# A hybrid decoder layer on one core: first weights loaded in quarters, the output gate's weights prepared in twos, convolutions one column later, half of the down projection's sums later

## The chip, the core and the metric

The kernel runs on one core of a Trainium2 chip. Five engines work beside each other and meet only through semaphores: TensorE (PE: matmuls, with its weight loads as PEld), VectorE (DVE), ScalarE (ACT), GpSimd (POOL) and SyncE (SP), which here issues nearly all transfers. Each engine takes its instructions strictly in the order in which the built program has them, so one that has to wait holds up all behind it. The metric is the time of one execution in microseconds on the device (us). Less is better.

## The reference, cut to what matters

```python
hn   = rmsnorm(x, attn_norm_w)                     # x: 1024 tokens x 1024
proj = hn @ w_in                                   # 3592 columns
da_q, da_k, da_v, ml_qk, ml_v, ml_o, ml_i, ml_f = split_projection(proj)
da   = rmsnorm(diff_attention(da_q, da_k, da_v, lam, slopes), diff_norm_w) * (1 - lam_init)
qk   = silu(causal_dwconv(ml_qk, mlstm_conv_w, mlstm_conv_b))     # width 4, 1024 channels
mq, mk = split(qk)
h    = mlstm_chunkwise(mq, mk * 128**-0.5, ml_v, ml_i + b_i, log_sigmoid(ml_f + b_f))
mix  = concat(da, sigmoid(ml_o) * rmsnorm(h, mlstm_norm_w))
x    = x + mix @ w_out
u    = causal_dwconv(rmsnorm(x, ffn_norm_w) @ w_up, ffn_conv_w, ffn_conv_b)
gate, up = split(u)
x    = x + (silu(gate) * up) @ w_down              # 2816 hidden channels
return rmsnorm(x, final_norm_w)
```

All of it is in float32. The change touches only the first fifth of the program, from the first load to the value projections. What it computes stays the same.

## The kernel before

A float32 factor is split into a high part (rounded to the matmul's type, `fp32r`, on ACT) and a low part (the rest, by a subtraction on DVE or POOL), and each product is three matmuls of 128x128 by 128x512: high x high, high x low, low x high. L158 to L160 (`mm3`) and L163 to L165 (`mm3b`) are these three. `split` (L115 and L116) makes the two parts of half a piece of weights, `split_x` (L212, L213) those of x.

The first fifth of the program runs in this order on PE:

1. eleven idle matmuls (L233) that keep PE at work until data arrives;
2. columns ct = 0 to 3 of `ml_qk` (queries of the mLSTM) for the first half of the tokens (`banks(0)`: the four accumulators in the two `big` tiles of PSUM), then for the second half (`banks(1)`: `mm`, `mm`, `sa`, `sb`). Each half is 4 columns x 8 slices kc of the model dimension x 3 matmuls. Before the change the order is: slices 0 to 3 of columns 0 and 1, slices 0 to 3 of columns 2 and 3, then slices 4 to 7 of all four. So the first load brings the first half (512 wide, 256 KB) of the weights of columns 0 and 1 (`col_halves`);
3. columns ct = 4 to 7 (keys), two halves each, in PSUM tiles that rotate (`rotate`);
4. the gate's pre-activations: 16 matmuls into a small PSUM tile `sb` and 16 into `sa` (L411), each copied to `gs` by L412;
5. the units of the output gate, `o_unit(0)` to `o_unit(7)`, then those of the attention's values, `v_unit(0)` to `v_unit(7)`, each 24 matmuls; `filler` puts small steps of the mLSTM's gates between them (eight transposes of `gs`, L477, after the second unit);
6. the projection of the mLSTM's values (first two tiles into `sa` and `sb`), and the chunks.

PSUM tiles `sa` and `sb` are taken in turn by `small`. A taker waits until the last holder was copied out: the copies of the keys are L393 on ACT, those of the queries L374 and L379.

Behind the matmuls run the convolutions of the 8 columns. M[ct] is first multiplied by the tokens' scale RB on DVE (L387, L394). `conv_qk(ct)` is one ACT instruction (L361) and three taps on DVE (L363, 128x1021 to 1023 elements) into an accumulator of the tag `ta` (4 buffers), and `silu_qk(ct)` one on ACT (L366).

POOL meanwhile makes sums of blocks of `w_down` for a later Strassen product. `down_sums` loads a pair (2 x 512 KB), makes 4 subtractions of 128x512 on POOL (L327), and `store_sums` writes the pair to memory (L333). There are 11 pairs. Their buffers are `vda` in the columns' loop, and `ta` in `late_sums`; `first_up_sums` does the same for two pairs of `w_up` (L341 to L344). Before the change a pair stands at ct = 1, 3, 4, 5, 6 and 7, at o_unit 1, 3, 5 and 7, and at v_unit 0.

Weights of 1024 columns go through one of two buffers `wf` and are split into two of eight tiles `w` (`wpiece`; `getw` takes the next of a list). `wo` are the four pieces of the output gate, `wv` those of the attention's values, and four more (`w_mv` too) are those of the mLSTM's values. A load into `wf` waits until its last content was split. A split waits until PE has used the `w` tile's last content.

A scheduler orders the instructions of every engine by dependencies and priorities, so an engine's order is not just that of the code. SP carries all loads and stores in one order: a store that waits for POOL holds up each load behind it.

Of the kernel before, what the change touches and what calls it, by code (L numbers as in the profile page):

```python
# [10 lines left out]
F32 = mybir.dt.float32  # L11
F32R = mybir.dt.float32r
I32 = mybir.dt.int32
AF = mybir.ActivationFunctionType
ALU = mybir.AluOpType
PSUM = bass.MemoryType.PSUM

P = 128
S = 1024
D = 1024  # L20
NT = S // P
KC = D // P
# [17 lines left out]
def tile_hybrid(ctx: ExitStack, tc: tile.TileContext, I: dict, out: bass.AP):  # L40
    nc = tc.nc
    V = nc.vector
    A = nc.scalar
# [23 lines left out]
    wp = Scope("wp")  # L67
# [34 lines left out]
    first = cp.tile([P, 1], F32, name="first")  # L102
# [9 lines left out]
    def split(dst, src, loeng, scale=None):  # L112

        if scale is None:
            A.activation(dst[:, 0, :], src, AF.Copy)  # L115
            loeng.tensor_tensor(dst[:, 1, :], src, dst[:, 0, :].bitcast(F32), op=ALU.subtract)  # L116
        else:
            A.activation(dst[:, 0, :], src, AF.Copy, scale=scale)
            V.scalar_tensor_tensor(dst[:, 1, :], src, scale, dst[:, 0, :].bitcast(F32), op0=ALU.mult, op1=ALU.subtract)

    def wtile():
        return wp.t([P, 2, 512], F32R, "w", 8)

    HV = (slice(0, 512), slice(512, 1024))
# [21 lines left out]
    def getw(ahead):  # L146
        n = used[0]
        used[0] += 1
        while len(made) < min(n + 1 + ahead, len(specs)):
            made.append(wpiece(*specs[len(made)]))  # L150
        return made[n]
# [48 lines left out]
    def load_x(i, hf, between=None):  # L200
        f = pa.t(XS, tag="ta", bufs=4)
        for c in ([slice(0, 1), slice(1, 2)] if between else [slice(0, 2)]):
            nc.sync.dma_start(f[:, c, :], I["xT"][:, 2 * i + c.start:2 * i + c.stop, HV[hf]])
            if between and c.start == 0:
                between()
        return f

    def split_x(i, hf, f):
        hi, lo = (px.t(XS, F32R, "xb", 16) for _ in range(2))
        for c in range(2):  # L210
            k = 2 * i + c
            A.activation(hi[:, c, :], f[:, c, :], AF.Copy, scale=anw[:, k:k + 1])  # L212
            V.scalar_tensor_tensor(lo[:, c, :], f[:, c, :], anw[:, k:k + 1], hi[:, c, :].bitcast(F32), op0=ALU.mult, op1=ALU.subtract)  # L213
        xb[i, hf] = hi, lo
# [15 lines left out]
    cw = {}  # L230
# [1 line left out]
    for _ in range(11):  # L232
        PE.matmul(idle, ones, ones, start=True, stop=True)  # L233

    def col_halves(half, *cts, first=False):

        f = wp.t([P, 1024], F32, "wf", 2)
        for ct, t in zip(cts, HV):
            nc.sync.dma_start(f[:, t], I["w_st"][ct][:, HV[half]])
            yield  # L240
            w = cw[ct, half] = wtile()
            if first:
                V.tensor_copy(w[:, 0, :], f[:, t])
                V.tensor_tensor(w[:, 1, :], f[:, t], w[:, 0, :].bitcast(F32), op=ALU.subtract)
            else:
                split(w, f[:, t], V)

    def col_piece(ct):
        cw[ct, 0], cw[ct, 1] = wpiece(I["w_st"][ct], None, V)

    g0 = col_halves(0, 0, 1, first=True)
    f = load_x(0, 0, lambda: next(g0))
    next(g0)
    split_x(0, 0, f)
    f = load_x(1, 0)
    split_x(1, 0, f)
    for _ in g0:
        pass
    for _ in col_halves(0, 2, 3):
        pass  # L260
    f = load_x(2, 0)
    split_x(2, 0, f)
    for _ in col_halves(1, 0, 1):
        pass
    f = load_x(3, 0)
    split_x(3, 0, f)
    for _ in col_halves(1, 2, 3):
        pass
    nc.sync.dma_start(cst, I["cst"])
    nc.sync.dma_start(wg, I["wg"])  # L270
    for i in range(4):
        f = load_x(i, 1)
# [39 lines left out]
    gs = pa.t([16, S], tag="gs")  # L312
# [6 lines left out]
    def down_sums(alloc=lambda: pr0.t([P, S], tag="vda", bufs=4), n=1):  # L319
        h0, h1 = HV  # L320
        for i in (pairs.pop(0) for _ in range(min(n, len(pairs)))):
            g, u = (alloc() for _ in range(2))
            for k, f in enumerate((g, u)):
                nc.sync.dma_start(f, I["w_down"][2 * i + k])
            for dst, x_, y in ((g[:, h1], g[:, h1], g[:, h0]), (u[:, h1], u[:, h1], g[:, h1]),
                               (u[:, h0], u[:, h0], u[:, h1]), (g[:, h0], u[:, h1], g[:, h0])):
                GP.tensor_tensor(dst, x_, y, op=ALU.subtract)  # L327
            dsum.append((i, g, u))

    def store_sums(n=1):  # L330
        for i, g, u in (dsum.pop(0) for _ in range(min(n, len(dsum)))):
            for k, f in enumerate((g, u)):
                nc.sync.dma_start(usum[i - NJ, k] if i >= NJ else wsum[i, k], f)  # L333

    def first_up_sums(j):

        h0, h1 = HV
        g, u = (pa.t([P, S], tag="ta", bufs=4) for _ in range(2))
        for k, f in enumerate((g, u)):
            nc.sync.dma_start(f, I["w_up"][j, k])  # L340
        GP.tensor_tensor(u[:, h0], g[:, h0], u[:, h0], op=ALU.subtract)  # L341
        GP.tensor_tensor(u[:, h1], u[:, h1], u[:, h0], op=ALU.subtract)
        GP.tensor_tensor(g[:, h0], u[:, h1], g[:, h0], op=ALU.add)
        GP.tensor_tensor(g[:, h1], g[:, h1], u[:, h1], op=ALU.subtract)  # L344
        dsum.append((NJ + j, g, u))

    def tok(tiles, tt):
        return tiles[tt // 2][:, tt % 2, :]

    def col_mm(ps, ct, kc, hf):  # L350
        k = slice(kc % 4 * P, (kc % 4 + 1) * P)
        w = cw[ct, kc // 4]
        mm3(ps, w[:, 0, k], w[:, 1, k], *xpart(kc, hf), kc == 0, kc == KC - 1)
# [3 lines left out]
    def conv_qk(ct):  # L357

        u = M[ct]
        acc = cacc[ct] = pa.t([P, S], tag="ta", bufs=4)  # L360
        A.activation(acc, u, AF.Identity, bias=mcb[:, ct:ct + 1], scale=mcw[:, ct, 3:4])  # L361
        for d in (1, 2, 3):
            V.scalar_tensor_tensor(acc[:, d:], u[:, :S - d], mcw[:, ct, 3 - d:4 - d], acc[:, d:], op0=ALU.mult, op1=ALU.add)  # L363

    def silu_qk(ct):
        A.activation(M[ct], cacc.pop(ct), AF.Silu)  # L366

    pss = banks(0)
    for cts, kcs in (((0, 1), range(4)), ((2, 3), range(4)), (range(4), range(4, 8))):
        for kc in kcs:  # L370
            for ct in cts:
                col_mm(pss[ct], ct, kc, 0)
    for ct in range(4):
        A.activation(M[ct][:, HV[0]], pss[ct], AF.Copy)  # L374
    pss = banks(1)
# [9 lines left out]
    stats()  # L385
    for ct in range(4):
        V.tensor_tensor(M[ct], M[ct], RB, op=ALU.mult)  # L387
    for ct in range(4, 8):
        for hf in range(2):
            ps = rotate(2 * ct + hf)  # L390
            for kc in range(KC):
                col_mm(ps, ct, kc, hf)
            A.activation(M[ct][:, HV[hf]], ps, AF.Copy)  # L393
        V.tensor_tensor(M[ct], M[ct], RB, op=ALU.mult)  # L394
        store_sums()
        down_sums()
        if ct == 4:
            col_piece(7)
        elif ct == 6:
            wo = [getw(0) for _ in range(4)]  # L400
        conv_qk(ct - 4)
        if ct > 4:
            silu_qk(ct - 5)
    mq, mk = M[0:4], M[4:8]


    for hf in range(2):
        gp = small([16, 512])
        for kc in range(KC):
            for m, x_ in enumerate(xpart(kc, hf)):  # L410
                PE.matmul(gp, wg16[:, kc, :], x_, start=(kc, m) == (0, 0), stop=(kc, m) == (KC - 1, 1))  # L411
        V.tensor_copy(gs[:, HV[hf]], gp)  # L412
    conv_qk(4)
    silu_qk(3)

    def mv_mm(ps, w, tt):
        for kc in range(KC):
# [6 lines left out]
    def late_sums():  # L424
        store_sums()
        down_sums(lambda: pa.t([P, S], tag="ta", bufs=4))
# [7 lines left out]

    def o_unit(tt):
        store_sums()
        if tt < 4:
            if tt < 3:
                conv_qk(5 + tt)
            silu_qk(4 + tt)  # L440
        if tt % 2:
            late_sums()
        if tt == 5:
            wv.extend(getw(0) for _ in range(4))
        if tt == NT - 1:
            return
        tts = (tt,) if tt < NT - 2 else (tt, tt + 1)
        pss = [rotate(k) for k in tts]
        mv_pair(pss, wo, tts)
        for ps, k in zip(pss, tts):  # L450
            A.activation(tok(Tt, k), ps, AF.Tanh, scale=rstdh[:, k:k + 1])

    def v_unit(tt):
        store_sums()
        if tt in (2, 4):
            first_up_sums(tt // 2 - 1)
        if tt == 0:
            late_sums()
            vda.extend(pr0.t([P, 2, 512], tag="vda", bufs=4) for _ in range(4))
        if tt == NT - 1:  # L460
            return
        tts = (tt,) if tt < NT - 2 else (tt, tt + 1)
        pss = [rotate(k + 2) for k in tts]
        mv_pair(pss, wv, tts)
        for ps, k in zip(pss, tts):
            A.activation(tok(vda, k), ps, AF.Copy, scale=rstd[:, k:k + 1])
# [184 lines left out]
    w = [getw(1) for _ in range(4)]  # L651
# [706 lines left out]
```

## Time and profile before

| | |
|---|---|
| median of 3 runs | 1214.32 us (1213.82 to 1214.63) |
| profiled execution, its own time | 1213.26 us |
| its span in the trace | 1211.5 us |
| PE busy / PEld busy | 1183.0 us (98%) / 973.3 us (80%) |
| DVE / ACT / POOL busy | 899.2 us (74%) / 571.0 us (47%) / 480.1 us (40%) |
| mean granted clock of TensorE | 0.995 of full speed |

The profiled execution took 1213.26 us by the clock that timed the runs; its trace spans 1211.5 us, and what is between them is start and end. It is one of the faster executions. Times in the text are microseconds from the start of the span. PE is busy nearly always, so the kernel can become faster only where PE waits or runs at a lower clock.

### The profile page before, as it was taken

The page shows a single profiled execution, that of the slowest core. Times are in us where ns is not written, and L with a number is a line of the kernel's source. Part 1 is how long each engine was busy: PE and PEld are TensorE (multiplying, and loading weights), DVE is VectorE, ACT ScalarE, POOL GpSimd, SP SyncE. Part 2 cuts the span into 40 slices and gives each one's busy share as a digit, 9 for nine tenths or more (in the row PEclk, how much of TensorE's full clock was granted, in tenths as well). Part 3 has the DMA queues.
Part 4 walks back from the last instruction along what each step waited for, and adds up shares of the span by engine and source line. Part 5 has one row for each costly group of instructions (what it writes and reads, how often), then busy time and mean ns, then how long its engine had stood idle before and what let it go on. Part 6 is the DMA issues. An engine that isn't in the chain of part 4 may idle for free.

```text
span 1211.5 us, 15939 instructions
## 1 busy us (share of the span) xinstructions
PE 1183.0 (98%) x5622; PEld 973.3 (80%) x5622; DVE 899.2 (74%) x1564; ACT 571.0 (47%) x1114; POOL 480.1 (40%) x364
## 2 busy tenths in 40 slices
PE   9998999999999999999999999999999999999996
PEld 7885788888778878888888888888888888888885
DVE  5598232566767777669998998788887878886694
ACT  6534323334666666344644444434344345544462
POOL 0475451003543431001198887888887600000000
PEclk9998999999999999999999999999999999999999
DMA  8755664124212243332322312222222169823223
GB/s 307 252 206 205 226 243 166 62 71 157 79 52 54 70 157 114 121 127 99 124 70 87 103 72 100 91 70 87 77 80 104 54 217 346 296 96 96 96 79 139
DMA packets 61743, 159.03 MB, mean 131 GB/s; under 512 B 6176, under 2 KB 10464, under 8 KB 61664
## 3 DMA queue, kind: packets, MB, share of 16 engines
q1 hardware_dynamic: 61232, 157.21, 38.0%
q8 instruction: 44, 0.72, 0.3%
q10 hardware_dynamic: 432, 0.82, 0.2%
q14 instruction: 35, 0.29, 0.1%
HBM read 116.02 MB, written 37.78 MB: 127 GB/s over the span
## 4 chain that ended last, share of the span: by engine, by line
PE 84%; DVE 5%; DMA 3%; ACT 3%; POOL 3%; issue 1%; SPq 1%; POOLq 0%; ACTq 0%; DVEq 0%
PE mm L160 6%; PE mm L158 6%; PE mm L159 6%; PE mm L163 5%; PE mm L164 5%; PE mm L165 5%; PE big L158 4%; PE big L160 4%; PE big L159 4%; PE big L164 4%; PE big L165 4%; PE big L163 4%; PE sb L777 3%; POOL vda L327 3%; PE sb L158 2%; PE sb L160 2%
## 5 line engine op out<-in xcount | busy, mean ns | idle before, releaser
L115 ACT ACTIVATE w<-wf 128x512 fp32r<-128x512 f32 x160 | 97.7, 624 | 142.3 <-POOL wf L999 33.6
L116 DVE TENSOR_TENSOR w<-wf,w 128x512 fp32r<-128x512 f32 x128 | 108.4, 858 | 27.9 <-ACT w L115 21.7
L1041 DVE SCALAR_TENSOR_TENSOR y<-x2b,fcw,y 128x1022 f32<-128x1022 f32 x44 | 91.8, 2125 | 0.0
L1040 DVE SCALAR_TENSOR_TENSOR y<-x2b,fcw,y 128x1023 f32<-128x1023 f32 x44 | 75.7, 1762 | 9.4 <-ACT y L1039 9.4
L116 POOL TENSOR_TENSOR w<-s,w 128x512 fp32r<-128x512 f32 x40 | 69.8, 1746 | 6.2 <-ACT w L115 6.2
L327 POOL TENSOR_TENSOR vda<-vda 128x512 f32<-128x512 f32 x24 | 46.6, 1958 | 63.7 <-DMA vda<-in_w_down_dram 62.9
L116 POOL TENSOR_TENSOR w<-wf,w 128x512 fp32r<-128x512 f32 x32 | 46.9, 1469 | 57.0 <-ACT w L115 47.2
L116 POOL TENSOR_TENSOR w<-wu,w 128x512 fp32r<-128x512 f32 x40 | 66.5, 1662 | 1.8 <-ACT w L115 1.8
L158 PE MATMUL mm<-xb,w 128*128 128x512 f32 x168 | 66.1, 394 | 0.0
L160 PE MATMUL mm<-xb,w 128*128 128x512 f32 x168 | 65.9, 392 | 0.0
L159 PE MATMUL mm<-xb,w 128*128 128x512 f32 x168 | 65.9, 392 | 0.0
L968 POOL TENSOR_TENSOR s<-wu 128x512 f32<-128x512 f32 x20 | 36.5, 1825 | 58.0 <-DMA wu<-in_w_up_dram 58.0
L752 DVE CUSTOM_DVE_ANT_0 s<-big,B 128x128 f32<-128x128 f32 (+7 forms) x64 | 47.6, 755 | 13.7 <-PE big L750 12.3
L1039 ACT ACTIVATE y<-x2b,fcw 128x1024 f32<-128x1024 f32 x44 | 52.3, 1237 | 9.6 <-DVE x2b L1030 8.4
L754 ACT ACTIVATE s<-s,mb 128x128 f32<-128x128 f32 (+7 forms) x64 | 49.3, 772 | 11.2 <-DVE mb L753 10.0
L163 PE MATMUL big<-w 128*128 128x512 f32 x132 | 51.5, 390 | 0.8 <-DVE x L1202 0.8
L164 PE MATMUL big<-w 128*128 128x512 f32 x132 | 51.4, 389 | 0.0
L165 PE MATMUL big<-w 128*128 128x512 f32 x132 | 51.3, 389 | 0.0
L115 ACT ACTIVATE w<-wu 128x512 fp32r<-128x512 f32 x48 | 29.7, 625 | 40.1 <-PE mm L160 10.7
L777 PEld LDWEIGHTS sb<-vda,aT 128*128 128x128 f32 x288 | 36.2, 190 | 15.4 <-ACT aT L774 14.6
L777 PE MATMUL sb<-vda,aT 128*128 128x128 f32 x288 | 44.2, 289 | 3.7 <-ACT aT L774 3.1
L115 ACT ACTIVATE w<-hb 128x512 fp32r<-128x512 f32 x41 | 25.8, 630 | 44.9 <-PE big L165 19.8
(514 smaller groups left out, 3769.8 us busy)
## 6 DMA issues: line engine op xcount, KB each, us to landing
wf<-in_w_up_dram SPq DMA_DIRECT2D x22, 512.0 KB, 4.5
actd<-y SPq DMA_DIRECT2D x21, 512.0 KB, 2.6
wu<-in_w_up_dram SPq DMA_DIRECT2D x20, 512.0 KB, 3.4
wf<-in_w_st_dram SPq DMA_DIRECT2D x12, 512.0 KB, 4.2
vda<-in_w_down_dram SPq DMA_DIRECT2D x12, 512.0 KB, 6.6
wsum<-vda SPq DMA_DIRECT2D x12, 512.0 KB, 3.0
wf<-in_w_mv_dram SPq DMA_DIRECT2D x12, 512.0 KB, 5.3
wf<-wsum SPq DMA_DIRECT2D x12, 512.0 KB, 3.4
```

Of the source, the lines that this page charges most:

```text
L115: A.activation(dst[:, 0, :], src, AF.Copy)
L116: loeng.tensor_tensor(dst[:, 1, :], src, dst[:, 0, :].bitcast(F32), op=ALU.subtract)
L158: PE.matmul(ps, sh, mh, start=first, stop=False)
L159: PE.matmul(ps, sh, ml, start=False, stop=False)
L160: PE.matmul(ps, sl, mh, start=False, stop=last)
L163: PE.matmul(ps, sh, w[:, 0, :], start=first, stop=False)
L164: PE.matmul(ps, sl, w[:, 0, :], start=False, stop=False)
L165: PE.matmul(ps, sh, w[:, 1, :], start=False, stop=last)
L327: GP.tensor_tensor(dst, x_, y, op=ALU.subtract)
L777: PE.matmul(ops, aT[:, b * P:(b + 1) * P], vda[k // 2][:, k % 2, h * P:(h + 1) * P], start=k == 0, stop=k == qt)
L1040: V.scalar_tensor_tensor(y[:, 1:], u[:, :S - 1], cw[:, 1:2], y[:, 1:], op0=ALU.mult, op1=ALU.add)
L1041: V.scalar_tensor_tensor(y[:, 2:], u[:, :S - 2], cw[:, 0:1], y[:, 2:], op0=ALU.mult, op1=ALU.add)
```

## The change

- **First weights in quarters.** Two steps of `first_quarter` load 256 columns (128 KB) of the weights of all four columns, instead of two steps of `col_halves` that load 512 columns of two of them. Every part is now split on ACT and DVE by `split`; the first two were made on DVE alone (L243, L244). PE takes the first half of the tokens slice by slice over all four columns.
- **Output gate's weights in twos.** Two pieces are prepared in the step ct = 6 and two in ct = 7, ahead of that step's sums and convolution, instead of four in ct = 6.
- **Convolutions a column later.** `conv_qk(0)` stands in the step ct = 5, not 4, and so on. All silus stand in the units of the output gate.
- **The copies of the gate's pre-activations** move from DVE (L412) to ACT.
- **Down sums.** Pairs now stand at ct = 1, 3, 5 and 7 and at o_unit 1, 3 and 5 (buffers `vda`), at o_unit 7 and at v_unit 0, 3 and 6 (`ta`).

```diff
-    g0 = col_halves(0, 0, 1, first=True)
+    def first_quarter(q):
+
+        f = wp.t([P, 1024], F32, "wf", 2)
+        for ct in range(4):
+            c, r = slice(256 * ct, 256 * (ct + 1)), slice(256 * q, 256 * (q + 1))
+            nc.sync.dma_start(f[:, c], I["w_st"][ct][:, r])
+            yield
+            if q == 0:
+                cw[ct, 0] = wtile()
+            split(cw[ct, 0][:, :, r], f[:, c], V)
+
+    g0 = first_quarter(0)
+    next(g0)
     f = load_x(0, 0, lambda: next(g0))
-    next(g0)
     split_x(0, 0, f)
+    for _ in g0:
+        pass
     f = load_x(1, 0)
     split_x(1, 0, f)
-    for _ in g0:
-        pass
-    for _ in col_halves(0, 2, 3):
+    for _ in first_quarter(1):
         pass
...
     pss = banks(0)
-    for cts, kcs in (((0, 1), range(4)), ((2, 3), range(4)), (range(4), range(4, 8))):
-        for kc in kcs:
-            for ct in cts:
-                col_mm(pss[ct], ct, kc, 0)
+    for kc in range(KC):
+        for ct in range(4):
+            col_mm(pss[ct], ct, kc, 0)
...
+    wo = []
     for ct in range(4, 8):
...
         V.tensor_tensor(M[ct], M[ct], RB, op=ALU.mult)
-        store_sums()
-        down_sums()
         if ct == 4:
             col_piece(7)
-        elif ct == 6:
-            wo = [getw(0) for _ in range(4)]
-        conv_qk(ct - 4)
+        elif ct > 5:
+            wo += [getw(0) for _ in range(2)]
+        if ct % 2:
+            store_sums()
+            down_sums()
         if ct > 4:
-            silu_qk(ct - 5)
+            conv_qk(ct - 5)
...
-        V.tensor_copy(gs[:, HV[hf]], gp)
-    conv_qk(4)
-    silu_qk(3)
+        A.activation(gs[:, HV[hf]], gp, AF.Copy)
...
     def o_unit(tt):
         store_sums()
-        if tt < 4:
-            if tt < 3:
-                conv_qk(5 + tt)
-            silu_qk(4 + tt)
-        if tt % 2:
+        if tt < 5:
+            conv_qk(3 + tt)
+        silu_qk(tt)
+        if tt in (1, 3, 5):
+            store_sums()
+            down_sums()
+        elif tt == NT - 1:
             late_sums()
...
     def v_unit(tt):
         store_sums()
         if tt in (2, 4):
             first_up_sums(tt // 2 - 1)
+        elif tt in (0, 3, 6):
+            late_sums()
         if tt == 0:
-            late_sums()
             vda.extend(pr0.t([P, 2, 512], tag="vda", bufs=4) for _ in range(4))
```

How the built program's order changes at three places:

SP, while PE works on columns 4 to 7. `wf<-in_w_st` is the piece of column 7, `wf<-in_w_mv` are the output gate's pieces, `vda<-in_w_down` and `wsum<-vda` the loads and stores of the sums. Before:

```order
L324 DMA vda<-in_w_down_dram 128x1024 x3
L333 DMA wsum<-vda 128x1024 x2
L129 DMA wf<-in_w_st_dram 128x1024
L333 DMA wsum<-vda 128x1024 x2
L324 DMA vda<-in_w_down_dram 128x1024 x4
L333 DMA wsum<-vda 128x1024 x2
L129 DMA wf<-in_w_mv_dram 128x1024 x2
```

After:

```order
L129 DMA wf<-in_w_st_dram 128x1024
L328 DMA vda<-in_w_down_dram 128x1024
L337 DMA wsum<-vda 128x1024 x2
L328 DMA vda<-in_w_down_dram 128x1024
L129 DMA wf<-in_w_mv_dram 128x1024 x2
L337 DMA wsum<-vda 128x1024 x2
L129 DMA wf<-in_w_mv_dram 128x1024
L328 DMA vda<-in_w_down_dram 128x1024 x4
L337 DMA wsum<-vda 128x1024
L129 DMA wf<-in_w_mv_dram 128x1024
```

The first two pieces of the output gate stood behind the loads of the fourth and fifth pair and the stores of the third and fourth; now they stand behind the stores of the second.

ACT, at the end of the columns, from the copy of `sa` (the first half of column 7) to the first units of the output gate (L451 before, L455 after). Before:

```order
L393 ACTIVATE mqk<-sa 128x512
L366 ACTIVATE mqk<-ta 128x1024
L115 ACTIVATE w<-wf 128x512 x2
L393 ACTIVATE mqk<-mm 128x512
L361 ACTIVATE ta<-mqk,par 128x1024
L366 ACTIVATE mqk<-ta 128x1024
L451 ACTIVATE Tt<-mm,rstdh 128x512
```

After:

```order
L397 ACTIVATE mqk<-sa 128x512
L370 ACTIVATE mqk<-ta 128x1024
L115 ACTIVATE w<-wf 128x512
L397 ACTIVATE mqk<-mm 128x512
L115 ACTIVATE w<-wf 128x512
L365 ACTIVATE ta<-mqk,par 128x1024
L416 ACTIVATE gs<-sb 16x512
L370 ACTIVATE mqk<-ta 128x1024
L416 ACTIVATE gs<-sa 16x512
L455 ACTIVATE Tt<-mm,rstdh 128x512
```

The scheduler has left the silus among the columns, and the second copy to `gs` now stands behind the last silu.

SP, while PE works on the attention's values. `mwd` and `DT` are small exchanges of the mLSTM's gates, the last `wf<-in_w_mv` rows the pieces of its values. Before:

```order
L340 DMA ta<-in_w_up_dram 128x1024 x3
L333 DMA usum<-ta 128x1024 x3
L522 DMA mwd<-s 32x128
L333 DMA usum<-ta 128x1024
L129 DMA wf<-in_w_mv_dram 128x1024
L522 DMA mwd<-s 32x128
L586 DMA DT<-mwd 128x512 x2
```

After:

```order
L328 DMA ta<-in_w_down_dram 128x1024 x2
L337 DMA usum<-ta 128x1024 x2
L337 DMA wsum<-ta 128x1024
L527 DMA mwd<-s 32x128
L337 DMA wsum<-ta 128x1024
L344 DMA ta<-in_w_up_dram 128x1024 x2
L527 DMA mwd<-s 32x128
L328 DMA ta<-in_w_down_dram 128x1024 x2
L337 DMA usum<-ta 128x1024 x2
L337 DMA wsum<-ta 128x1024 x2
L129 DMA wf<-in_w_mv_dram 128x1024
L591 DMA DT<-mwd 128x512 x2
```

Two pairs of down sums now stand here with their loads and stores, ahead of the second piece of the mLSTM's values. From there on the program's order is as before.

## Rows read from the trace of the kernel before

**Rows 1.** The page's first part: busy time, share and instructions of each engine.
```profile
PE 1183.0 (98%) x5622; PEld 973.3 (80%) x5622; DVE 899.2 (74%) x1564; ACT 571.0 (47%) x1114; POOL 480.1 (40%) x364
```

**Rows 2.** The waits of PE: total us, times, longest us.
```profile
PE sa L411 <- ACT mqk L393: 5.9, 1, 5.9
...
PE big L158 <- DVE w L243: 1.7, 2, 0.9
```

**Rows 3.** Timeline of the first 10 us, PE and DVE: start, us, instruction, idle time before it.
```profile
0.99 4.21 PE L233 MATMUL sa<-ones 128*128 128x128 f32 x22 [0.99 <-POOL wprev L544]
...
7.51 0.43 DVE L243 CAST w<-wf 128x512 fp32r<-128x512 f32 x1 [0.24 <-DMA wf<-in_w_st_dram]
...
9.06 0.39 PE L158 MATMUL big<-xb,w 128*128 128x512 f32 x1
9.29 0.39 PE L159 MATMUL big<-xb,w 128*128 128x512 f32 x1
```

**Rows 4.** Timeline of PE, 95 to 217 us.
```profile
96.09 3.88 PE L411 MATMUL sb<-xb,wg 128*16 128x512 f32 x16
105.90 5.71 PE L411 MATMUL sa<-xb,wg 128*16 128x512 f32 x16 [5.92 <-ACT mqk L393]
...
124.86 0.42 PE L477 MATMUL sb<-cst,gs 16*128 16x16 f32 x4 [2.02 <-DVE gs L412]
...
210.97 0.39 PE L165 MATMUL sa<-w,xb 128*128 128x512 f32 x1
```

**Rows 5.** Windows of 10 us: busy us of PE, PEld, DVE, ACT, POOL; PEclk.
```profile
100.00:110.00 10.00, 4.10 (x10) 1.42 (x11) 9.49 (x7) 5.36 (x7) 6.49 (x4) 0.66 0.47 191
```

**Rows 6.** Timeline of ACT, 60 to 110 us.
```profile
91.53 2.43 ACT L115 ACTIVATE w<-wf 128x512 fp32r<-128x512 f32 x4 [5.07 <-DMA wf<-in_w_mv_dram]
...
105.27 0.57 ACT L393 ACTIVATE mqk<-sa 128x512 f32<-128x512 f32 x1
```

**Rows 7.** Timeline of DVE, 50 to 210 us.
```profile
53.51 6.83 DVE L387 TENSOR_TENSOR mqk<-mqk,RB 128x1024 f32<-128x1024 f32 x4 [3.73 <-ACT RB L302]
60.27 9.00 DVE L363 SCALAR_TENSOR_TENSOR ta<-mqk,par,ta 128x1023 f32<-128x1023 f32 x4
...
92.19 3.62 DVE L116 TENSOR_TENSOR w<-wf,w 128x512 fp32r<-128x512 f32 x4 [2.35 <-ACT w L115]
95.74 4.85 DVE L363 SCALAR_TENSOR_TENSOR ta<-mqk,par,ta 128x1022 f32<-128x1022 f32 x4
...
102.87 1.22 DVE L394 TENSOR_TENSOR mqk<-mqk,RB 128x1024 f32<-128x1024 f32 x1
...
207.88 0.69 DVE L116 TENSOR_TENSOR w<-wf,w 128x512 fp32r<-128x512 f32 x1 [0.98 <-ACT w L115]
```

**Rows 8.** Timeline of POOL, 50 to 190 us.
```profile
55.05 15.36 POOL L327 TENSOR_TENSOR vda<-vda 128x512 f32<-128x512 f32 x7 [4.13 <-DMA vda<-in_w_down_dram]
77.83 16.23 POOL L327 TENSOR_TENSOR vda<-vda 128x512 f32<-128x512 f32 x8 [7.42 <-DMA vda<-in_w_down_dram]
...
166.26 3.90 POOL L327 TENSOR_TENSOR ta<-ta 128x512 f32<-128x512 f32 x3 [6.85 <-DMA ta<-in_w_down_dram]
...
185.72 1.29 POOL L344 TENSOR_TENSOR ta<-ta 128x512 f32<-128x512 f32 x1
```

**Rows 9.** Timeline of SP's queue of transfers, 60 to 215 us.
```profile
86.94 1.24 SPq L129 DMA_DIRECT2D wf<-in_w_mv_dram  x2
...
170.56 4.96 SPq L340 DMA_DIRECT2D ta<-in_w_up_dram  x3
...
187.42 0.42 SPq L129 DMA_DIRECT2D wf<-in_w_mv_dram  x1
```

**Rows 10.** Transfers issued from 145 to 190 us: count, KB each, median us to landing.
```profile
wsum<-ta SPq DMA_DIRECT2D x4, 512.0 KB, 5.0
ta<-in_w_up_dram SPq DMA_DIRECT2D x4, 512.0 KB, 4.5
usum<-ta SPq DMA_DIRECT2D x4, 512.0 KB, 2.6
```

**Rows 11.** The same view, transfers issued from 186 to 215 us.
```profile
wf<-in_w_mv_dram SPq DMA_DIRECT2D x3, 512.0 KB, 3.5
```

More of the change, by code (lines that the diff above doesn't have):

```diff
@@ L233, in tile_hybrid, with col_halves @@
         PE.matmul(idle, ones, ones, start=True, stop=True)
-    def col_halves(half, *cts, first=False):
+    def col_halves(half, *cts):
         f = wp.t([P, 1024], F32, "wf", 2)
@@ L239, in col_halves @@
             nc.sync.dma_start(f[:, t], I["w_st"][ct][:, HV[half]])
-            yield
             w = cw[ct, half] = wtile()
[L242 to L246, printed above, removed]
+            split(w, f[:, t], V)
     def col_piece(ct):
         cw[ct, 0], cw[ct, 1] = wpiece(I["w_st"][ct], None, V)
-    g0 = col_halves(0, 0, 1, first=True)
+    def first_quarter(q):
[9 more added lines that the diff above has]
+    next(g0)
     f = load_x(0, 0, lambda: next(g0))
-    next(g0)
     split_x(0, 0, f)
+    for _ in g0:
+        pass
     f = load_x(1, 0)
     split_x(1, 0, f)
-    for _ in g0:
-        pass
-    for _ in col_halves(0, 2, 3):
+    for _ in first_quarter(1):
         pass
@@ L262, in tile_hybrid @@
     split_x(2, 0, f)
-    for _ in col_halves(1, 0, 1):
-        pass
+    col_halves(1, 0, 1)
     f = load_x(3, 0)
     split_x(3, 0, f)
-    for _ in col_halves(1, 2, 3):
-        pass
+    col_halves(1, 2, 3)
     nc.sync.dma_start(cst, I["cst"])
```

## The prediction

> **What bounds the kernel.** I read the page first, then the waits of PE, then the timelines around each wait. PE is busy for 98% of the span [rows 1], and two of its waits lie where the change works: 5.9 us before the second half of the gate's matmuls, which wait for ACT's copy out of `sa`, and 1.7 us at the start [rows 2]. The reader should see three more things. After the 5.92 us wait the 16 matmuls take 5.71 us, where the 16 before it took 3.88; the granted clock is 0.66 on average from 100 to 110 us, that is, TensorE was put from its level of 2.4 GHz to 1.2 for a part of it [rows 4, 5]. That costs another 1.83 us. And the transposes of `gs` wait 2.02 us at 124.86. From there to the first bank of the mLSTM's values I found no wait of PE in the trace. So 5.92 + 1.83 + 2.02 + 1.7 = 11.5 us is all that the change can win here.
>
> Why was the copy late? SP issued the output gate's first two pieces only at 86.94, since stores of sums that waited for POOL stood ahead of them [rows 9]. ACT, which takes its work in order, waited 5.07 us for their landing until 91.53, with finished columns uncopied behind it [rows 6]. DVE in turn waited 2.35 us for ACT [rows 7]. But DVE is the longer queue: from 53.51 it works until its multiplication ends at 102.87 + 1.22 = 104.09; then ACT makes a convolution step and the copy at 105.27, done at 105.84. 50.6 us on DVE with 2.35 idle leave 48.2 us of work. It is the true bound of this wait.
>
> **First weights in quarters.** Matmuls that follow each other start 0.23 us apart, as at 9.06 and 9.29 [rows 3]. By 9.06 PE had done six, so it runs as if it had started at 9.06 - 6 x 0.227 = 7.70. The idle matmuls end at 0.99 + 4.21 = 5.20. In the new order the four quarters of slice 0 and the two slices of x are the same 1,024 KB that lay ahead of 7.51, when the second half-piece landed [rows 3]; so the last quarter is there at about 7.5. Its halves cost half of 2.43/4 on ACT [rows 6] and half of 0.69 on DVE [rows 7]: 0.3 and 0.35 us. PE then has work for 24 matmuls, of which nine need only the first three quarters, and has done 13 by about 8.7: as if from 5.75. That is a gain of 1.95 at most; 0 if the quarters land no earlier than halves did. I take 1.7. The eight more splits and four more issues lie in the gaps before x's next slices; without that cover they would cost some 2.6 us on ACT.
>
> The Trainium skill ("DMA: Bandwidth & Descriptors", Rules for kernel authors) speaks against it: it wants transfers large, 1 MiB and more, and says small ones should be joined. Taken strictly the quarters would win nothing, and the sum below would be worse by 1.7. Here it is a question of order, not of size, as the same bytes come; whether 128 KB lands slower no row shows.
>
> **Weights in twos, convolutions later, fewer sums in the columns' loop.** The order of the built program shows what is left of it. The silus are still among the columns. Ahead of the multiplication that releases the copy of `sa`, DVE has what it had: 7 multiplications, 18 taps, 7 low parts. What goes is the wait: the first pieces' loads now stand behind the second pair's stores. POOL made that pair's last sum at 55.05 + 3 x 2.19 = 61.6 [rows 8], 25 us ahead of 86.94, so neither ACT nor DVE should wait for these weights again. New end on DVE: 53.51 - 1.7 + 48.2 = 100.0, if its operations take as long as before.
>
> That "if" needs POOL. Four taps took 9.00 us while POOL was at work and 4.85 when it was not [rows 7, 8]: 2.25 and 1.21 each. POOL made 7 + 8 = 15 sums within DVE's stretch. Now the third to fifth pair land a little later, but I count 15 again before 100 (3 of the second pair, 4 each of the third to fifth). So DVE's 48.2 us stay; if the fifth pair's four fell behind the stretch, DVE would be 4 x 1.04 = 4.2 us sooner.
>
> The copy of `sa` then ends at 100.0 + 1.75 = 101.8, and PE asks for it at 96.09 + 3.88 - 1.7 = 98.3: a wait of 3.5 us instead of 5.92. Whether the clock falls is open: it did after 5.92 us, but the matmuls behind the 2.02 us wait came at the full pace again. So 0 to 1.83 us; it does not count, because of the next wait.
>
> **Copies of `gs` on ACT.** Before, 124.86 - 104.09 = 20.8 us went by from DVE's multiplication to the transposes. On that path two DVE copies go (0.6 each, by the nearest row, ACT's 0.57), and a silu of 1024 columns (about 1.1, twice a half split) and a copy (0.6) come on ACT: the second copy now stands behind the last silu, which waits for the same three taps. Sum +0.5. The transposes go on at 100.0 + 20.8 + 0.5 = 121.3. PE would be there by 119 even at the low clock. So this wait decides, and **the gain at 125 us is 124.86 - 121.3 = 3.6 us**; with a little less of POOL on the last taps, 3.8. Bounds: 1.2, if DVE waits for weights as before; 8, with the fifth pair's sums elsewhere.
>
> **Sums spread to the values' units.** Here I expect the gain to be given back. On the clock of before: POOL's last down sum ended at 166.26 + 3.90 = 170.16, SP asked for `w_up` at 170.56, eight sums ended at 185.72 + 1.29 = 187.0, and at 187.42 SP issued the second piece of the mLSTM's values [rows 8, 9]. Its buffers and tiles would have let it wait until about 199, so it had time. Now two more down pairs stand in the same queue ahead of it. Eight sums at 3.90/3 = 1.3 are 10.4 us. The second pair of `w_up` can only be asked for behind the last store of the pair before it, so POOL idles for an issue and a load, 0.8 + 4.5 [rows 10]. About 1.4 us are won earlier, since the eighth pair's sums lie long before (my estimate). The second piece leaves SP at 187.4 + 10.4 + 5.3 - 1.4 = 201.7.
>
> Who waits for it: it lands about 206 and its second low part is made at about 209, with DT's exponentials between; only then its buffer is free for the fourth piece, which takes 3.5 us to land [rows 11] and about 2.6 to be split (two high parts with a copy between them, one low part): 215.2. The last matmul of the first bank stood at 210.97 [rows 4], and the low part that it needs was done at 207.88 + 0.69 = 208.57 [rows 7], 2.4 us early. So PE loses 215.2 - 211.0 = 4.2 us. Both clocks move with PE, so the gain before does not change it. Bounds: 0, if stores take 2.6 and not 5.0 us and three loads 3.5 and not 4.5 [rows 10, 11], which is 5.4 us; 8, if two more stores take 5.0 and the clock falls as at 105.9 (+1.83). The stores of `w_up`'s sums were short, so I take 3.4.
>
> **Sum.** 3.8 - 3.4 = 0.4 us faster: 1213.26 - 0.4 = 1212.9 for the profiled execution's time, and 1214.32 - 0.4 = 1213.9 for the median, which lies 1.06 above it. That is no change: 0.2% is 2.4 us, about what a measurement of this kernel tells from none.
>
> **Rivals.**
> - *Faster: the late queue is hidden.* POOL idles much of the time from 110 to 190 us, and the pieces had 2.4 us to spare; with short links the loss is 0 to 1.2. Against it: SP's order is fixed, and eight sums cannot take less than 10 us. Time: 1214.3 - 3.8 + 0.6 = 1211.1; with POOL's fifth pair off DVE's stretch as well, 1207.
> - *Slower: the value weights stop PE in one long piece.* If the second piece leaves SP after 204 on the clock of before, the wait passes 6 us, as long as the one behind which the clock fell; then 6.2 + 1.8 - 3.8 = 4.2 us are lost: 1218.5. The mixed lengths of stores [rows 10] speak for it; that the four pieces come one by one, with matmuls between, speaks against it.
> - *The twos do nothing.* The silus stayed where they were, and DVE's work is the same. If DVE also waits as long, only 1.2 us are won there: 1214.3 - 1.2 + 3.4 = 1216.5. Within 0.2%.
>
> **Chances.** No change 0.46 (the forecast 0.40, the twos that do nothing 0.06), faster 0.33, slower 0.21. The range goes from 1210.2, within the first rival, to 1217.4, short of the second.
>
> **What would show it.** The first matmul of weights at 5.2 to 5.5 us and 13 matmuls by 9; DVE without a wait for weights from 52 to 100 us; the wait before the gate's second half at 3 to 4 us; the transposes' wait still there, on ACT now; and a new wait of PE before the first bank of the mLSTM's values, for a split, with SP issuing `wf<-in_w_mv` behind `wsum` stores at about 197 on its own clock. I am wrong if that last wait is missing, or if it is over 6 us, or if the gain by 125 us is under 2 or over 6.

## The result: slower by 0.63%

The changed kernel takes 1222.04 us in the median of six runs (1219.42 to 1224.59), the kernel before 1214.13 beside it (1213.28 to 1215.77). The ratio is 1.0063, with a 95% interval of 1.0049 to 1.0077: 7.7 us slower, where I had forecast no change and a range from 1210.2 to 1217.4. The profiled execution's span is 1220.0 us, 8.5 more than before.

PE's part of the page and its longest waits in the kernel after:

```profile
PE 1188.7 (97%) x5622; PEld 976.0 (80%) x5622; DVE 895.2 (73%) x1564; ACT 574.0 (47%) x1122; POOL 477.0 (39%) x364
```

```profile
PE sa L415 <- ACT mqk L397: 5.0, 1, 5.0
PE sa L163 <- ACT w L115: 3.1, 2, 2.8
...
PE sb L482 <- ACT gs L416: 2.0, 1, 2.0
...
PE sa L165 <- DVE w L116: 1.1, 1, 1.1
...
PE big L158 <- ACT w L115: 1.0, 1, 1.0
```

Beside [rows 2] two waits for split weights into `sa` are new (L163 and L165, 4.2 us together): they lie in the first bank of the mLSTM's values, that is, the 24 matmuls of its first output tile. The wait before the gate's second half has become 5.0, not 3.5. To see where time goes, one reads when PE comes to the same instruction. The timeline of PE after, at the places of [rows 4]:

```profile
95.04 3.88 PE L415 MATMUL sb<-xb,wg 128*16 128x512 f32 x16
103.89 5.14 PE L415 MATMUL sa<-xb,wg 128*16 128x512 f32 x16 [4.96 <-ACT mqk L397]
...
122.69 0.42 PE L482 MATMUL sb<-cst,gs 16*128 16x16 f32 x4 [1.98 <-ACT gs L416]
...
146.52 0.60 PE L513 MATMUL sa<-cst,lf 128*4 128x128 f32 x4
...
209.45 0.79 PE L163 MATMUL sa<-w,xb 128*128 128x512 f32 x1 [2.77 <-ACT w L115]
...
211.79 0.80 PE L165 MATMUL sa<-w,xb 128*128 128x512 f32 x1 [1.12 <-DVE w L116]
...
219.48 0.40 PE L165 MATMUL sa<-w,xb 128*128 128x512 f32 x1
...
225.18 0.60 PE L604 MATMUL sa<-cst,mqk 128*128 128x128 f32 x4
```

and two places of before that [rows 4] did not show, the gate's rows (small transposes of the mLSTM's gates, which I use as a mark of where PE is) and the first transposes of the chunks:

```profile
147.14 0.60 PE L508 MATMUL sa<-cst,lf 128*4 128x128 f32 x4
...
216.64 0.60 PE L599 MATMUL sa<-cst,mqk 128*128 128x128 f32 x4
```

The changed kernel is ahead by 1.05 us at the gate's first half (96.09 to 95.04), by 2.17 at the transposes, by 0.62 at the gate's rows, and then behind by 8.54 at 225 us. All is lost between the last two: 9.2 us. Behind that the two kernels run alike to the end.

Windows of 10 us after (columns as in [rows 5]):

```profile
120.00:130.00 10.00, 8.02 (x34) 6.23 (x33) 2.44 (x8) 6.98 (x9) 2.54 (x2) 0.83 0.71 261
...
200.00:210.00 10.00, 7.23 (x31) 5.70 (x30) 0.00 (x0) 0.63 (x1) 4.07 (x6) 0.95 0.62 223
210.00:220.00 10.00, 8.54 (x20) 4.94 (x19) 6.07 (x12) 6.34 (x16) 0.00 (x0) 0.53 0.54 193
```

The granted clock was at its lower level, 1.2 of 2.4 GHz, for a part of the time behind the transposes (0.83 on average from 120 to 130 us), and for nearly all of 210 to 220 us, in the bank of the values (0.53). The first explains why 2.17 us became 0.62: from 123.91 us matmuls took 0.63 us each, not 0.39. Whether the second costs anything is a question for an experiment: it lies in a stretch in which PE waits for weights.

The queue of SP after, from 120 us, beside [rows 9]:

```profile
123.83 28.98 SPq L328 DMA_DIRECT2D ta<-in_w_down_dram  x3
...
186.24 1.29 SPq L344 DMA_DIRECT2D ta<-in_w_up_dram  x2
...
202.86 1.57 SPq L337 DMA_DIRECT2D wsum<-ta  x2
204.47 0.45 SPq L129 DMA_DIRECT2D wf<-in_w_mv_dram  x1
205.02 1.26 SPq L591 DMA_DIRECT2D DT<-mwd  x2
...
206.80 6.71 SPq L129 DMA_DIRECT2D wf<-in_w_mv_dram  x2
```

POOL behind it, and ACT and DVE in front of PE:

```profile
180.53 5.27 POOL L331 TENSOR_TENSOR ta<-ta 128x512 f32<-128x512 f32 x4
192.67 1.28 POOL L345 TENSOR_TENSOR ta<-ta 128x512 f32<-128x512 f32 x1 [6.87 <-DMA ta<-in_w_up_dram]
...
198.36 5.71 POOL L331 TENSOR_TENSOR ta<-ta 128x512 f32<-128x512 f32 x4
```

```profile
208.77 0.63 ACT L115 ACTIVATE w<-wf 128x512 fp32r<-128x512 f32 x1 [10.88 <-DMA wf<-in_w_mv_dram]
211.17 0.69 ACT L594 ACTIVATE DT<-DT,gg 128x128 f32<-128x128 f32 x2 [1.78 <-DVE DT L592]
211.77 0.61 ACT L115 ACTIVATE w<-wf 128x512 fp32r<-128x512 f32 x1
```

```profile
52.45 5.74 DVE L390 TENSOR_TENSOR mqk<-mqk,RB 128x1024 f32<-128x1024 f32 x4 [1.31 <-ACT RB L306]
...
83.55 13.48 DVE L367 SCALAR_TENSOR_TENSOR ta<-mqk,par,ta 128x1021 f32<-128x1021 f32 x6
...
100.86 1.21 DVE L398 TENSOR_TENSOR mqk<-mqk,RB 128x1024 f32<-128x1024 f32 x1
...
210.45 0.69 DVE L592 TENSOR_TENSOR DT<-DT,cst 128x512 f32<-128x512 f32 x1 [11.50 <-DMA DT<-mwd]
...
218.39 0.69 DVE L116 TENSOR_TENSOR w<-wf,w 128x512 fp32r<-128x512 f32 x1 [0.40 <-ACT w L115]
```

Read from below: the last low part of the fourth piece is done at 218.39 + 0.69 = 219.08, and PE's last matmul of the bank starts at 219.48. The fourth piece needed the buffer of the second, whose second half ACT could split only at 211.77, behind `DT`, which DVE got at 210.45. Piece and `DT` were issued at 204.47 and 205.02, behind the last store, whose sums POOL ended at 204.07; and POOL had stood for 6.87 us for the second pair of `w_up`.

### The profile page after: what moved, and what is told of

Its sections match the earlier page's. It is cut to its first block, busy times and chain, and to the rows that moved or that the text cites. A ratio compares the mean times of both kernels' runs of the same rounds, so it can differ in the third digit from the quotient of the medians.

```text
span 1220.0 us, 15955 instructions
## 1 busy us (share of the span) xinstructions
PE 1188.7 (97%) x5622; PEld 976.0 (80%) x5622; DVE 895.2 (73%) x1564; ACT 574.0 (47%) x1122; POOL 477.0 (39%) x364
## 4 chain that ended last, share of the span: by engine, by line
PE 80%; DVE 8%; DMA 4%; ACT 3%; POOL 2%; issue 2%; SPq 0%; DVEq 0%; POOLq 0%; ACTq 0%
PE mm L160 6%; PE mm L158 6%; PE mm L159 6%; PE big L158 4%; PE big L160 4%; PE big L159 4%; PE mm L163 4%; PE mm L164 4%; PE mm L165 4%; PE big L163 3%; PE big L164 3%; PE big L165 3%; DVE ta L367 3%; PE sb L782 3%; PE sb L158 2%; PE sb L160 2%
## 5 line engine op out<-in xcount | busy, mean ns | idle before, releaser
L115 ACT ACTIVATE w<-wf 128x512 fp32r<-128x512 f32 (+1 forms) x166 | 99.8, 614 | 144.4 <-POOL wf L1004 34.3
L116 DVE TENSOR_TENSOR w<-wf,w 128x512 fp32r<-128x512 f32 (+1 forms) x134 | 111.0, 838 | 34.0 <-ACT w L115 26.0
L331 POOL TENSOR_TENSOR vda<-vda 128x512 f32<-128x512 f32 x28 | 54.3, 1958 | 66.8 <-DMA vda<-in_w_down_dram 62.5
L757 DVE CUSTOM_DVE_ANT_0 s<-big,B 128x128 f32<-128x128 f32 (+7 forms) x64 | 47.6, 755 | 13.4 <-PE big L755 11.9
L163 PE MATMUL big<-w 128*128 128x512 f32 x132 | 51.5, 390 | 0.8 <-DVE x L1207 0.8
L165 PE MATMUL big<-w 128*128 128x512 f32 x132 | 51.3, 389 | 0.0
L115 ACT ACTIVATE w<-wu 128x512 fp32r<-128x512 f32 x48 | 29.7, 625 | 40.2 <-PE mm L160 10.7
```

The lines of the kernel that those rows point to most:

```text
L163: PE.matmul(ps, sh, w[:, 0, :], start=first, stop=False)
L165: PE.matmul(ps, sh, w[:, 1, :], start=False, stop=last)
```

## The experiments

Each ratio is to runs of the kernel before that were taken beside the experiment on the same chip.

**Both late pairs early.** In the kernel after:

```diff
-        if tt in (1, 3, 5):
+        if 0 < tt < 6:
             store_sums()
             down_sums()
...
-        elif tt in (0, 3, 6):
+        elif tt == 0:
             late_sums()
```

> Theory Q (queue): all that the changed kernel loses, it loses because the two pairs of down sums at v_unit 3 and 6 keep SP from issuing the second piece of the mLSTM's values until 204.5 us. With these two pairs at o_unit 2 and 4 instead (tiles vda), SP issues it at about 187, PE has no wait in the first bank of the values, and the kernel takes 1213.5 us (1212.0 to 1214.5). Rival P (pieces): the loss comes from another part of the change (weights in twos, copies on ACT, quarters), so it stays: 1220 us or more.

1211.68 us, ratio 0.9975 (0.9965 to 0.9986): 3.0 us faster than before, 10.7 faster than the changed kernel, and a little under the range of theory Q. SP issued the second piece early again:

```profile
185.88 0.42 SPq L129 DMA_DIRECT2D wf<-in_w_mv_dram  x1
```

and PE had no wait in that bank. The rest of the change loses nothing; by the ratios, the two late pairs cost 10.7 us. The trace is of its slowest execution (1215.85): there it is 0.89 us ahead of before at the first chunk (215.75 against 216.64). Where the rest of the 3.0 us comes from is not shown.

**The late pairs alone.** In the kernel before:

```diff
-        store_sums()
-        down_sums()
+        if ct % 2:
+            store_sums()
+            down_sums()
...
             first_up_sums(tt // 2 - 1)
+        elif tt in (3, 6):
+            late_sums()
```

> The kernel before, with the pairs of ct = 4 and 6 taken out and two pairs put at v_unit 3 and 6. Theory Q: SP issues the second piece at about 204, PE waits in the first bank of the values and runs at half clock behind that, some 9 us lost from 200 to 220 us; the fewer sums among the columns give back 0 to 4: 1219 to 1223 us. Rival P: 1211 to 1215 us, since nothing else of the change is in it.

1217.29 us, ratio 1.0019 (1.0008 to 1.003): slower, but less than I expected. Its profiled execution (1214.52, its fastest run) shows both signs:

```profile
101.92 3.88 PE L412 MATMUL sa<-xb,wg 128*16 128x512 f32 x16 [1.97 <-ACT mqk L393]
...
117.62 0.42 PE L480 MATMUL sb<-cst,gs 16*128 16x16 f32 x4 [0.56 <-DVE gs L413]
...
217.56 0.60 PE L602 MATMUL sa<-cst,mqk 128*128 128x128 f32 x4
```

At the transposes it is 7.24 us ahead of before, at 217 us 0.92 behind: a loss of 8.2 in the tail, with SP's second piece at 197.33 on a clock on which PE runs 7.3 us early. So the loss needs nothing but the two late pairs. The gain in front was a surprise: taking pairs from the columns is worth far more there than the changed kernel got.

**Quarters alone.** `first_quarter` and the order of matmuls in the kernel before, nothing else.

> The kernel before with the first weights in quarters and nothing else. If the 1.05 us that the changed kernel has won by the gate's matmuls is carried through, 1213.1 us. Rival: the copy of sa is set by DVE's work, which does not start sooner, so the wait before the gate's second half grows by the same 1 us: 1214.1 us.

1213.98 us, ratio 0.9992 (0.9982 to 1.0002). Inconclusive. In its profiled execution PE waited 1.77 us at 9.10 for the split of a quarter, and the gate's first half starts at 96.16, as before; in those of the other kernels with quarters it starts at 94.2 to 95.6. So this trace does not decide between the two expectations.

**One late pair.** The kernel after with only the pair of v_unit 6 moved, to o_unit 4:

```diff
-        elif tt in (0, 3, 6):
+        elif tt in (0, 3):
             late_sums()
```

> The changed kernel with only the pair of v_unit 6 moved to o_unit 4; that of v_unit 3 stays. Theory Q: the queue has slack (the second piece can wait until about 199 us), and one pair makes it 7 to 12 us later than 187, so 194 to 199: no wait or one under 1 us, 1213.5 us (1212.0 to 1215.0). Rival (each late pair costs half of the loss): about 1218 us.

1220.13 us, ratio 1.0044 (1.0028 to 1.0061). My theory was too narrow. Moving one pair wins back only 2.3 us, though the second piece is not late at all, so neither expectation came. From the gate's rows (144.45) to the first chunk (221.39) it loses 7.4 us against before. SP:

```profile
186.33 0.42 SPq L129 DMA_DIRECT2D wf<-in_w_mv_dram  x1
193.37 2.94 SPq L337 DMA_DIRECT2D usum<-ta  x2
196.40 3.26 SPq L591 DMA_DIRECT2D DT<-mwd  x2
```

ACT and PE:

```profile
201.61 0.70 ACT L594 ACTIVATE DT<-DT,gg 128x128 f32<-128x128 f32 x2 [8.64 <-DVE DT L592]
202.21 0.62 ACT L115 ACTIVATE w<-wf 128x512 fp32r<-128x512 f32 x1
```

```profile
205.36 0.50 PE L165 MATMUL sa<-w,xb 128*128 128x512 f32 x1 [1.74 <-DVE w L116]
...
210.65 0.51 PE L163 MATMUL sa<-w,xb 128*128 128x512 f32 x1 [2.34 <-ACT w L115]
```

The piece left at 186.33 and took 5.5 us to land, but ACT stood 8.64 us for `DT` (a tile of the mLSTM's first chunk), which is ahead of the splits in its order, and `DT`'s load stood behind the last store of sums. So two things hang on that store: the piece and the first chunk's `DT`. One late pair delays `DT`, the second pair the piece as well.

**Idle matmuls in the wait.** The kernel after with twelve matmuls of `ones` ahead of the second piece's in the first bank:

```diff
         for kc in range(KC):
+            if idle and kc == 2:
+                d = mmps()
+                for _ in range(idle):
+                    PE.matmul(d[:, 0:P], ones, ones, start=True, stop=True)
```

> The changed kernel with twelve idle matmuls of 128x128 by 128x128 on PE (0.38 us each by the eleven at the start, 4.6 us in all) between the first and the second piece of the first bank of the mLSTM's values, where PE waited 4.2 us in three parts and then ran at half clock. Clock theory: the 5 us that the half clock costs are lost by themselves; PE now stays at work, the clock stays at 1.0, and 5 us come back: 1217.5 us. Chain theory: PE's pace there does not matter, since the last matmuls need the fourth piece, whose last low part was made at 219.1 us whatever PE does; the clock stays up, PE waits for the later pieces instead, and the time stays at 1222 us (1220.5 to 1223).

1221.65 us, ratio 1.0053 (1.0038 to 1.0068): as the changed kernel. PE:

```profile
205.33 2.84 PE L423 MATMUL mm<-ones 128*128 128x128 f32 x24
208.74 0.50 PE L163 MATMUL sa<-w,xb 128*128 128x512 f32 x1 [0.57 <-ACT w L115]
...
214.35 0.63 PE L165 MATMUL sa<-w,xb 128*128 128x512 f32 x1
...
218.17 0.50 PE L165 MATMUL sa<-w,xb 128*128 128x512 f32 x1
```

The first wait is nearly filled, and part of the bank ran at full pace (0.39 to 0.40 a matmul, not 0.63), yet the bank ends only 1.3 us sooner, in a run in which PE was 1.0 us ahead already at the gate's rows. The test is not clean, as the clock still fell for part of the bank, but the traces give a bound. The last low part of the fourth piece is done at 218.11 here and the last matmul of the bank starts at 218.17; in the changed kernel these are 219.08 and 219.48. So the bank ends when the fourth piece is split, and the lower clock cost the changed kernel at most the 0.4 us between.

**Six pairs' sums left out.** In the kernel after, POOL's subtractions of the second to seventh pair are missing:

```diff
-                GP.tensor_tensor(dst, x_, y, op=ALU.subtract)
+                if not 1 <= i <= 6:
+                    GP.tensor_tensor(dst, x_, y, op=ALU.subtract)
```

> The changed kernel without POOL's subtractions of the second to seventh pair (they are left out; loads and stores stay). Contention theory: DVE's taps and products from 52 to 102 us take their short time (1.21 each), its work shrinks by 13 to 15 us to about 35, PE does not wait before the gate's second half nor before the transposes, and 125 us come 8 to 10 us sooner than in the changed kernel. Rival: DVE is held by ACT and the columns instead, and PE still waits over 2 us.

One execution, 1211.83 us; I read its stretches and not its time. DVE and PE:

```profile
52.05 4.63 DVE L391 TENSOR_TENSOR mqk<-mqk,RB 128x1024 f32<-128x1024 f32 x4 [2.00 <-ACT RB L306]
...
85.08 1.22 DVE L399 TENSOR_TENSOR mqk<-mqk,RB 128x1024 f32<-128x1024 f32 x1
```

```profile
98.37 3.87 PE L416 MATMUL sa<-xb,wg 128*16 128x512 f32 x16
...
113.09 0.66 PE L483 MATMUL sb<-cst,gs 16*128 16x16 f32 x8
...
199.60 0.80 PE L163 MATMUL sa<-w,xb 128*128 128x512 f32 x1 [3.96 <-ACT w L115]
```

PE waits neither at the gate nor at the transposes, which come 9.6 us sooner. DVE's stretch, from the first product with RB to the one that releases `sa`, is 86.30 - 52.05 = 34.2 us. With it the stretch can be laid out over four runs, by the number of POOL's sums inside it:

| run | POOL's sums inside | stretch, us | 34.2 + 1.03 x sums |
|---|---|---|---|
| six pairs' sums left out | 0 | 34.2 | 34.2 |
| late pairs alone | 12 | 46.6 | 46.6 |
| after | 15 | 49.6 | 49.7 |
| sums behind the columns, kernel after | 16 | 51.1 | 50.7 |

Each sum that takes POOL 1.3 us by itself (5.27 for four from 180.53) costs DVE 1.03 when both are at work. The other seven runs of changed kernels lie within 0.5 us of the same line: 15 sums and 49.7 to 49.8 us in three, 12 and 46.6 in three, 16 and 50.2 with quarters alone. So these two engines do not meet only through semaphores. The Trainium skill ("SBUF — State Buffer", SBUF: two separate sides) says that they share a pair of ports under an exclusive lock, which a DVE operation with two inputs in SBUF and a POOL operation that reads SBUF both need, and that the one that comes second waits for the whole operation of the other; the table agrees that DVE loses time for each sum, four fifths of a sum here.

The tail's loss stands here too, though PE is 10.9 us early: the second piece left at 193.84, 10.6 us sooner than in the kernel after, and from the gate's rows to the first chunk 9.2 us are lost again (135.59 and 214.27 against 147.14 and 216.64 before). The queue moves with PE, since it stands for a `ta` tile of the gate's rows, until 153 us in the changed kernel and until 142 us here.

**Sums behind the columns.** Two kernels with the sums at ct = 1, 3, 5, 7, at o_unit 1 to 5 and 7 in `ta`, and at v_unit 0. First in the kernel before with quarters:

```diff
-        store_sums()
-        down_sums()
+        if ct in (5, 7):
+            store_sums()
+            down_sums()
...
-        if tt % 2:
+        if tt in (1, 2, 3, 4, 5, 7):
             late_sums()
```

> The kernel before with quarters, and the down sums at ct = 1, 3, 5, 7, at o_unit 1, 2, 3, 4, 5, 7 (all in ta, so that their loads come behind the convolutions' accumulators) and at v_unit 0; none later. If POOL's sums inside DVE's stretch set the wait before the gate, and late pairs the loss at 205 us, it has the first 125 us of the kernel with two late pairs (7.2 us sooner there than before) and no loss behind: 1207 us (1205 to 1209). Rival: the two pairs more in the output gate's units delay the attention's value weights or the last convolutions, and half is given back: 1210 to 1212.

1221.18 us, ratio 1.0043 (1.0027 to 1.0059). The transposes came at 116.32, 8.5 us sooner than before, but the first chunk 7.0 us later (223.67). Those 15.6 us went at the next weights:

```profile
162.25 0.79 PE L163 MATMUL sa<-w,xb 128*128 128x512 f32 x1 [7.98 <-ACT w L115]
```

PE stood for the third piece of the attention's values, issued at 154.64 behind two more pairs, and 1.66 us more at 167.55. The two waits are 9.6 us. The other 5.9, by difference, go with the granted clock:

```profile
160.00:170.00 10.00, 6.05 (x12) 3.40 (x12) 4.10 (x4) 3.46 (x6) 4.94 (x5) 0.50 0.81 288
170.00:180.00 10.00, 10.00 (x42) 7.99 (x41) 1.98 (x7) 1.61 (x3) 4.62 (x5) 0.73 0.83 302
```

So the lower clock costs little only where PE would wait for weights anyway, as in the bank of the mLSTM's values. Then in the kernel after, with the same line in `o_unit` in place of its two branches and no pair at v_unit 3 and 6:

> The changed kernel with the sums placed as in the run with the sums behind the columns (o_unit 1, 2, 3, 4, 5, 7 in ta, v_unit 0). It still has the twos, the convolutions a column later and the copies on ACT. If these matter nothing and the place of the sums is all, it is as fast as that run: 1207 us. If they cost of themselves what the changed kernel did not win in its first 125 us, 1210 to 1212.

1212.68 us, ratio 0.9985 (0.9976 to 0.9994), faster than before, but without that front: it waits 6.5 us before the gate's second half and is 2.08 us ahead at the transposes, not 8.5. POOL's first sum in `ta` starts at 87.22 there, at 94.47 in the run before it and at 95.19 in the run with the late pairs alone, and 16 sums lie in DVE's stretch (table). SP issued the first load into `ta` at 75.67, against 89.94 in the run before it. That these buffers come free earlier because the convolutions stand a column later is my reading; no run separates it from the other parts of the change.

**Held buffers.** Two tries to have the front of the late pairs alone without late pairs: the two pairs go into `vda` at o_unit 2 and 4, and ACT first writes a column of these buffers behind the output gate's second unit.

```diff
+    held = [pr0.t([P, S], tag="vda", bufs=4) for _ in range(4)]
...
+        if tt == 1:
+            for f in held:
+                A.activation(f[:, 0:1], tok(Tt, 1)[:, 0:1], AF.Copy)
```

> The kernel before with quarters and the down sums of the kernel with two late pairs (ct = 1, 3, 5, 7, o_unit 1, 3, 5, 7 and v_unit 0), the two pairs left over in vda at o_unit 2 and 4; these buffers are first written in one column by ACT behind the output gate's second unit, so that POOL gets the two pairs only behind 118 us, in the stretch from 131 to 147 us in which it had nothing to do. If POOL's sums in DVE's stretch, late pairs, and pairs ahead of the attention's value weights are the three things that cost time, none is left: the transposes at 116.3 us as in the run with the sums behind the columns, 8.5 us sooner than before, and 1206 us (1204 to 1209). Rival: the third piece of the attention's values, which SP issued at 147 us in the kernel with two late pairs, is again held behind the stores of these pairs, and PE waits for it as it did at 162 us in the run with the sums behind the columns: 1209 to 1215.

1217.77 us, ratio 1.0013 (1.0001 to 1.0024). The transposes came at 117.34, and the rival was right: the third piece left at 152.40 and PE stood 4.03 us for it until 159.52. In the second try two of the buffers are written behind ACT's first copy out of column 7, for a pair at o_unit 0, and two behind the first unit, for one at o_unit 2.

> As the run with held buffers, but the two pairs in vda do not come together: one is held until ACT has copied the first half of column 8 of the projection (about 109 us), the other until the output gate's first unit (about 118 us), so that their loads stand between those of the pairs in ta. POOL then has four pairs from about 115 to 140 us, and SP is free again for the third piece of the attention's values at about 147 us, as in the kernel with two late pairs. If the order of SP's queue ahead of that piece is what the run with held buffers lost by, PE has no wait at 155 to 165 us and none at 200: 1206.5 us (1204.5 to 1209), 8 us under before. Rival: the first of these pairs runs beside the last taps and gives back 2 us or more at the transposes, or the piece is late again: 1209 to 1215.

1219.09 us, ratio 1.0035 (1.0023 to 1.0047): the piece left at 152.31, and PE stood 3.70 us until 158.50. Both lose 12 us from the transposes to the first chunk; some 6 of these are waits, and the granted clock is 0.50 from 160 to 170 us in both. The best version found is the changed kernel with both late pairs early, at 0.9975.

## Why the prediction was wrong

- **What bounds the kernel: right.** DVE's stretch, not the weights of the output gate, set the wait before the gate's second half. DVE waited for no weights after, and PE's wait shrank by only 1.0 us. With quarters alone, where the weights are not prepared in twos, DVE did not wait for them either, and its stretch took 50.2 us; so what the twos do by themselves is not shown.
- **First weights in quarters: 1.7 predicted, 1.05 in the trace.** PE began at 5.02, but waited 0.98 us at 7.99 for the third quarter, which landed no earlier than the half before (ACT split it at 7.52), and the parts of a quarter took 0.42 us on each engine, not 0.3 and 0.35. By itself the edit is within what the runs can tell.
- **The wait before the gate's second half: 3.5 predicted, 4.96 measured.** DVE's product ended at 102.07, not 100.0. I had counted 15 sums of POOL and there were 15; but I took the 48.2 us of before as they were. In the kernel before, two of the 15 ran while DVE stood idle from 89.84 to 92.19 (POOL was busy for 2.27 of these 2.35 us) and so cost DVE nothing: 13 sums by the line of the table make 47.6 us, and DVE worked for 48. Without the wait all 15 count, and the stretch is 49.6. What I had booked as won with the wait came back as contention with POOL.
- **Copies of `gs` on ACT: right.** 20.6 us from DVE's product to the transposes, 21.3 predicted. The gain there was 2.17 (3.8 predicted). I left out that the clock would fall behind this wait, as it had not before; 1.55 us more went, and 0.62 was left of the 3.8.
- **Sums spread to the values' units: this step failed.** The mechanism was the one described, link by link; the size was not. I took a loss of 3.4, with 0 to 8 as its bounds; it was 9.2. On the clock of before (the time after plus the 0.62 us by which PE is ahead there) the second piece should leave SP at 201.7; it left at 204.47, which is 205.1. POOL idled 6.87 us for the pair of `w_up`, not 5.3, and the last eight sums took 204.07 - 192.67 = 11.4 us, not 10.4: 2.6 us. Of the 1.4 us that I had taken off, 0.6 came, by difference. The second low part was done 8.7 us after the issue, not 7.3: `DT` was issued behind the piece, and ACT's first exponentials of it, for which ACT stood 1.78 us, are ahead of the split of the piece's second half. The fourth piece then took 6.0 (6.2 predicted). I had also shaded 4.2 down to 3.4 "since the stores of `w_up`'s sums were short"; no run bears that out. The gain in front (1.6 less), the clock (1.55) and the tail (5.8 more) make up the 8.9 us between the forecast, 0.4 ahead, and the 8.5 behind.
- **"Both clocks move with PE": right**, by the runs with six pairs' sums left out and with late pairs alone.
- **The rivals.** The slower one had the side right, and its condition (the piece behind 204 on the clock of before) held. Its price did not: I added a half clock to a long wait; the waits were three and short, the longest 2.77 us, the clock fell, and it cost at most 0.4 us of its own. The chain to the fourth piece is the price. My signs of being wrong asked for a wait over 6 us or a gain under 2 or over 6, and none of them came: the loss has to be read from when PE passes the same instruction, not from its longest wait. The faster rival's short links did not come, and that of the twos asked for a wait of DVE that was not there.

What stays open: how much of the tail would go if `DT` had another place. It lies in a pool of tiles (`pb`) that is opened when the pool with the sums' `ta` is closed. In the run with one late pair its two loads took 3.26 us in the queue behind the last store's issue, and 1.6 of these were a wait for a store `usum<-ta` to land, so SP's order is not all. Another place was not tried.

## What to carry to other kernels

Work that no engine on the path needs still sits in a queue with work that it does need: before moving it later, find the last thing on the same queue and in the same buffers that has a due time, and count the queue's links as serial (load, sums, store), each at its measured length. Where two engines slow each other, count the operations of the one inside the stretch of the other; here 1.03 us for each told the stretches of the eleven changed kernels within 0.5 us. An idle time of one engine may be where the other runs undisturbed, so closing it wins less than its length. A stretch won in front is kept only if the queue behind has room: three kernels that won 7.5 to 8.5 us by 117 us gave it back, and more, at the next weights and to the lower clock behind them.

## Not expected of the hardware

- Two waits of PE of the same length, 2.02 us before and 1.98 after, at the same transposes: behind the first the granted clock stayed at 1.00 (2.4 GHz), behind the second it was 0.83 over 120 to 130 us, at 1.2 GHz for a part of it. Ahead of both PE had worked for 17 us since the gate's second half. The length of a wait alone does not tell whether the clock falls.
- The idle matmuls took 2.84 us for 24 at 205 us (0.12 each), and 4.27 for 22 at the start (0.19), both in stretches with the clock at 1.00. I had sized the filler by the latter.
